# Row sums of the softmax in the third layer turned on TensorE, and evacuations given to ScalarE

## Chip, cores and metric

The kernel runs on one core of one Trainium2 chip. The metric is the device time of one execution in microseconds (us); before the change the median of three runs is 2798.11 us.

## What is computed

Four token mixers over one sequence of 1024 positions with 1024 features, all in float32: gated linear attention, dilated sliding-window attention, differential attention and multi-head latent attention, each followed by gating, an output projection and a residual with its norm. The third is the one that matters most here:

```python
def _diff_attention(h, positions, w_in, lam..., subln_g, w_out, lambda_init):
    q, k, v, z = split(h @ w_in)               # 8 heads, q and k of 2 x 64, v of 128
    q, k = _rope(q, positions), _rope(k, positions)
    ...
        sc = einsum('bqhcd,bkhcd->bhcqk', qb, k) * scale
        p = softmax(sc, axis=-1)
        p = p[:, :, 0] - lam * p[:, :, 1]
        o = einsum('bhqk,bkhd->bqhd', p, v)
    o = _rmsnorm(o, subln_g) * (1.0 - lambda_init)
    return (o * silu(z)) @ w_out
```

Layers three and four scale and shift their input by `silu(c) @ ada_w + ada_b` and multiply by a gate from the same product.

## The kernel before

Every matmul of float32 data is split into a high and a low part, and three products (high by high, low by high, high by low; L165 to L167) are added in PSUM. TensorE's order of work is written out by hand: the main loop of a layer issues its own matmuls and, by a credit in ns, gives time to a list of small units (`Fill`) that prepare what comes next: projections of the next head (`u_q`, `u_k`), gates (`u_gate`, L250), values (`u_v`) and the modulation (`u_ada`, L557: eight multiply-adds on VectorE, L575 and L577, over a 2 MB weight piece, then two matmuls against ones at L583). The other engines' order is set by the framework's scheduler from the data dependences and a simulated time. SyncE (SP in the profile) issues all transfers, in order.

A unit's result leaves PSUM by a copy: the gates' on ScalarE for the first half of the sequence and on VectorE for the second (L254), the second layer's values on VectorE and ScalarE in turn (L959), the third layer's likewise (L1285), the fourth layer's low-rank projections on VectorE (L1485). Before each of the layers two to four a stage (`pre`) runs such units with no attention beside them. Value weights come as `wvraw`, are cast on ScalarE (L204, `wvhi`) and their low part made on VectorE (`wvlo`, L150).

The third layer (`da`) walks 8 heads by 8 query tiles of 128 rows, 64 iterations `i`, and two more that finish. An iteration turns the probabilities of tile i-2 (`attend`, L1240: eight PE transposes of 128x128, copied to `PTh` on ScalarE and `PTl` on VectorE), finishes the softmax difference of tile i-1 (`combine`, L1440 to L1443: reciprocal, factor, P[0] + factor P[1]), computes the scores of tile i (L1420), their maxima on VectorE (L1424) and exponentials on ScalarE (L1426). On every odd iteration `pv` (L1358) multiplies a pair of tiles by the values, writes the unnormalised output to DRAM (`d_o`) and `norm` (L1377) writes a row of sums of squares (`d_ms`).

The outputs are not divided by the softmax sum: that goes into the RMS norm. For this the sum of the first softmax, `dsum` (128 rows on partitions, one column for each tile), is written to DRAM (`d_dn`), four columns at a time, and `factors` (L1245) loads sums of squares and softmax sums back as 128x4 pieces (`vr`), for all heads at once, and makes the factors on VectorE by an integer guess and four Newton steps (L1254 to L1265). It is called from `norm` at two places (head 6 last tile, head 7 second pair) and once in the boundary behind the layer. The write is

```python
nc.sync.dma_start(self.dnd[h][:, half(t // 4)].rearrange("o (f p) -> (o p) f", p=128), dsum[:, t - 3:t + 1])
```

in `combine`, that is, 512 elements of 4 bytes, each to an address of its own.

Of the kernel before, what the change touches and what calls it, by code (L numbers as in the profile page):

```python
# [8 lines left out]
F32 = mybir.dt.float32  # L9
# [128 lines left out]
class Kern:  # L138
# [111 lines left out]
    def u_gate(self, h, src, pool, halves=(0, 1), w=None):  # L250

        def evac(hf, s, ps):
            z = self.wp.tile([128, 512], F32, name="zt", bufs=2)
            (self.nc.vector.tensor_copy if hf else self.nc.scalar.copy)(z, ps)  # L254
            self.nc.sync.dma_start(self.zd[h][hf], z)
        return self.u_t(("g", h, halves[0]), (src, h), evac, halves=halves, w=w)
# [6 lines left out]
    def build(self):  # L263
        tc, nc, A = self.tc, self.nc, self.A
        with ExitStack() as ctx:
# [9 lines left out]
            self.ones = cp.tile([128, 128], F32, name="ones")  # L275
            self.ones_r = cp.tile([128, 128], F32R, name="ones_r")
            self.cv = cp.tile([128, 4], F32, name="cv")
# [6 lines left out]
            nc.vector.memset(self.ones_r.bitcast(F32), 1.0)  # L284
# [34 lines left out]
    def gla(self):  # L319
        tc, nc, A = self.tc, self.nc, self.A  # L320
        V, S, G, T = nc.vector, nc.scalar, nc.gpsimd, nc.tensor
        with ExitStack() as ctx:
# [22 lines left out]
            def u_g(h, halves=(0, 1)):  # L345
                return self.u_gate(h, "gla_wg", gp, halves)
# [334 lines left out]
    def boundary(self, name, wo, res, res_out, warm, ln=None, gate=None, mod=None, normed=False):  # L681
# [151 lines left out]
        for hf, off, n in parts:  # L833
            s = slice(hf * 512 + off, hf * 512 + off + n)
            for kt in range(2 if hf == 0 else 6 if final else 3, 8) if off == 0 else ():
                if normed and hf == 0 and kt == 7:
                    self.factors(bo, [(7, 1)])
# [90 lines left out]
    def swa(self, before):  # L928
# [6 lines left out]
        with ExitStack() as ctx:  # L935
# [13 lines left out]
            with tc.tile_pool(name="swv", bufs=1, reuse_waits="tile") as vp:  # L949
# [7 lines left out]
                def u_vs(g, sts):  # L957
                    def evac(st, ps):
                        (S.copy if st % 2 else V.tensor_copy)(Vt[g][:, st, :], ps)  # L959
# [225 lines left out]
            def after(h, g):  # L1185
# [13 lines left out]
                if g == 2:  # L1199
                    if h == 2:  # L1200
                        fill.add(u_kk(1, 0))
                    fill.add(self.u_gate(h, "swa_wg", ap, (0, 1) if h > 2 else (1,)))
# [42 lines left out]
    def factors(self, pool, hs):  # L1245

        nc, V = self.nc, self.nc.vector
# [6 lines left out]
        V.scalar_tensor_tensor(e, e, 128.0 * 1e-6, e, op0=OP.mult, op1=OP.mult)  # L1254
        V.tensor_tensor(t, t, e, op=OP.add)
        V.tensor_scalar(t, t, 1.0 / 128.0, None, op0=OP.mult)

        yi = y.bitcast(I32)
        V.tensor_scalar(yi, t.bitcast(I32), 1, None, op0=OP.logical_shift_right)
        V.tensor_scalar(yi, yi, -1.0, float(0x5f3759df), op0=OP.mult, op1=OP.add)  # L1260
        V.tensor_scalar(t, t, -0.5, None, op0=OP.mult)
        for _ in range(4):
            V.tensor_tensor(e, y, y, op=OP.mult)
            V.tensor_tensor(e, e, t, op=OP.mult)
            V.scalar_tensor_tensor(y, e, 1.5, y, op0=OP.add, op1=OP.mult)  # L1265
        for n, (g, hf) in enumerate(hs):
            nc.sync.dma_start(flat(self.rsd[g], hf), y[:, 4 * n:4 * n + 4])

    def da(self, before):
# [3 lines left out]
        with ExitStack() as ctx:  # L1273
            with tc.tile_pool(name="dav", bufs=1, reuse_waits="tile") as vp:
# [8 lines left out]
                def evac_v(pr, st, ps):  # L1283
                    t = vp.tile([128, 256], F32, name="vs", bufs=3)
                    (S.copy if st % 2 else V.tensor_copy)(t, ps)  # L1285
# [11 lines left out]
                with tc.tile_pool(name="ada1", bufs=1, side="right", reuse_waits="tile") as gp:  # L1297
                    ada = [self.u_ada(gp, *it) for it in ((1, 0), (1, 1), (1, 2), (1, 3), (0, 4), (0, 5))]
                    pre.add(u_vs(0, range(4, 8)), u_vs(1, range(4, 5)), ada[0], u_vs(1, range(5, 8)), ada[1], u_vs(2, range(0, 4)), ada[2], u_vs(2, range(4, 8)), ada[3], u_vs(3, range(0, 4)), ada[4], u_vs(3, range(4, 8)), ada[5])
# [50 lines left out]
            zs = [self.u_gate(h, "da_wz", dp, (hf,)) for hf, h in [(1, h) for h in range(3)] +  # L1350
# [7 lines left out]
            def pv(qb):  # L1358
                h, qb4 = divmod(qb, 4)
                s = slice(qb4 % 2 * 256, qb4 % 2 * 256 + 256)  # L1360
                o = self.mmp.tile([128, 256], F32, name="mm")
                vh, vl = VH[h]
                PTh, PTl = PT.pop(qb)
                for j in range(8):
# [6 lines left out]
                nc.sync.dma_start(self.od[h][qb4 // 2][:, s], y)  # L1371
                sq = dp.tile([128, 256], F32, name="sq")
# [3 lines left out]
            def norm(h, qb4, sq):  # L1376
# [5 lines left out]
                if (h, qb4) in FACT:  # L1382
                    self.factors(dp, FACT[h, qb4])

            FACT = {(6, 3): [(h, hf) for h in range(7) for hf in range(2)], (7, 1): [(7, 0)]}
            nrm, comb = None, []
            for i in range(64 + 2):
# [7 lines left out]
                if comb:  # L1395
                    comb.pop()()
                if i < 64:
# [37 lines left out]
                    if nrm and j % 2:  # L1435
                        norm(*nrm)
# [3 lines left out]
                    def combine(dn=dn, d0=d0, P=P, h=h, t=t, dsum=dsum):  # L1440
# [340 lines left out]
```

## Time and profile before

| | before |
|---|---|
| median of 3 runs | 2798.11 us (2795.3 to 2800.18) |
| the profiled execution: its time | 2794.63 us |
| its span in the profile | 2792.9 us |
| mean granted TensorE clock, as a share of the full one | 0.985 |
| busy: TensorE / VectorE / ScalarE / GpSimd | 95% / 68% / 48% / 11% |

The profile has a page for the whole span and views of any stretch: what ran when on an engine, how long it sat idle before and what released it, busy times and granted clock by window. An idle time in square brackets stands just ahead of the instruction that it ends before.

### The profile page before, as it was taken

How to read it: one execution, taken by the hardware profiler on the slowest of the kernel's cores; microseconds unless marked ns; L12 is line 12 of the kernel's file. 1: busy time of each engine (PE TensorE's matmuls, PEld its weight loads, DVE VectorE, ACT ScalarE, POOL GpSimd, SP SyncE). 2: the span in 40 equal slices, each digit the busy share in tenths (PEclk: the TensorE clock that was granted, in tenths of full speed). 3: DMA queues.
4: the chain of work that ended last, by engine and by line, in shares of the span. 5: the costliest groups of instructions: out<-in, count | busy, mean ns of one | idle time of the engine just before them, and what ended most of it. 6: DMA issues, size and time to landing. Idle time of an engine off the chain costs nothing.

```text
span 2792.9 us, 39308 instructions
## 1 busy us (share of the span) xinstructions
PE 2660.9 (95%) x14788; PEld 2234.5 (80%) x14788; DVE 1890.0 (68%) x3478; ACT 1349.2 (48%) x2492; POOL 314.6 (11%) x224
## 2 busy tenths in 40 slices
PE   8999999998999999988999999998799899999998
PEld 7889988887778878776897877786578688888878
DVE  7776547567666666667657788886576627777785
ACT  5444345426344434347515766765445415554563
POOL 0000000000000000000015656664000000000000
PEclk9999999999999999999999999999799999999999
DMA  5310155654111111154642432342275220100143
GB/s 206 107 43 32 49 180 182 210 176 144 50 42 50 46 47 53 50 185 145 228 165 74 63 67 61 66 55 62 90 266 170 68 70 23 33 27 29 39 172 110
DMA packets 163926, 274.70 MB, mean 98 GB/s; under 512 B 32948, under 2 KB 82388, under 8 KB 162072
## 3 DMA queue, kind: packets, MB, share of 16 engines
q1 hardware_dynamic: 163736, 272.19, 31.7%
q8 instruction: 116, 1.90, 0.3%
q14 instruction: 74, 0.61, 0.1%
HBM read 195.48 MB, written 66.17 MB: 94 GB/s over the span
## 4 chain that ended last, share of the span: by engine, by line
PE 67%; DVE 14%; DMA 7%; ACT 7%; issue 3%; SPq 1%; POOL 1%; ACTq 0%; DVEq 0%; POOLq 0%
PE mm L165 14%; PE mm L166 14%; PE mm L167 14%; PE pt L1240 3%; PE sc L1420 3%; PE sc L1657 2%; PE sc L1049 2%; PE lv L489 1%; PE pt L1153 1%; PE sc L166 1%; PE sc L165 1%; PE sc L167 1%; DVE den L1424 1%; PE mm L1623 1%; DVE wlo L150 1%
## 5 line engine op out<-in xcount | busy, mean ns | idle before, releaser
L165 PE MATMUL mm<-xh,whi 128*128 128x512 f32 x1456 | 613.3, 421 | 18.0 <-DVE t L911 6.0
L167 PE MATMUL mm<-xh,wlo 128*128 128x512 f32 x1456 | 574.0, 394 | 2.5 <-POOL wlo L150 1.6
L166 PE MATMUL mm<-xl,whi 128*128 128x512 f32 x1456 | 574.0, 394 | 1.7 <-DVE xl L150 1.7
L165 PEld LDWEIGHTS mm<-xh,whi 128*128 128x128 f32 x1456 | 277.6, 191 | 75.5 <-DVE t L911 7.3
L167 PEld LDWEIGHTS mm<-xh,wlo 128*128 128x128 f32 x1456 | 275.8, 189 | 64.4 <-POOL wlo L150 2.5
L166 PEld LDWEIGHTS mm<-xl,whi 128*128 128x128 f32 x1456 | 277.6, 191 | 52.9 <-DVE xl L150 4.0
L150 POOL TENSOR_TENSOR wlo<-wraw,whi 128x1024 fp32r<-128x1024 f32 x29 | 70.6, 2435 | 1334.9 <-ACT whi L192 1332.9
L165 PE MATMUL mm<-wvhi,xh 128*128 128x256 f32 x704 | 204.6, 291 | 4.8 <-DVE V L959 3.0
L192 ACT CAST whi<-wraw 128x1024 fp32r<-128x1024 f32 (+2 forms) x141 | 135.9, 964 | 138.3 <-PE mm L166 128.9
L167 PE MATMUL mm<-wvhi,xl 128*128 128x256 f32 x704 | 199.2, 283 | 0.1
L166 PE MATMUL mm<-wvlo,xh 128*128 128x256 f32 x704 | 198.6, 282 | 0.0
L1426 ACT ACTIVATE P<-sc,den 128x1024 f32<-128x1024 f32 x128 | 142.9, 1117 | 113.4 <-DVE den L1424 112.8
L1424 DVE TENSOR_REDUCE den<-sc 128x1 f32<-128x1024 f32 x128 | 153.5, 1212 | 3.5 <-PE sc L1420 3.5
L150 DVE TENSOR_TENSOR wlo<-wraw,whi 128x1024 fp32r<-128x1024 f32 (+2 forms) x113 | 123.5, 1093 | 43.8 <-ACT whi L192 40.7
L1043 ACT ACTIVATE P<-P,nm 128x128 f32<-128x128 f32 (+1 forms) x192 | 84.9, 443 | 124.5 <-DVE nm L1041 124.2
L165 PEld LDWEIGHTS mm<-wvhi,xh 128*128 128x128 f32 x704 | 134.0, 190 | 9.9 <-DVE V L959 3.2
L166 PEld LDWEIGHTS mm<-wvlo,xh 128*128 128x128 f32 x704 | 134.5, 191 | 1.3 <-issue 1.0
L167 PEld LDWEIGHTS mm<-wvhi,xl 128*128 128x128 f32 x704 | 133.9, 190 | 0.4 <-DVE xl L150 0.4
L165 PE MATMUL mm<-oh,xh 128*128 128x512 f32 (+1 forms) x336 | 126.1, 375 | 0.3 <-ACT oh L796 0.3
L166 PE MATMUL mm<-ol,xh 128*128 128x512 f32 (+1 forms) x336 | 124.2, 370 | 2.0 <-DVE ol L150 2.0
L167 PE MATMUL mm<-oh,xl 128*128 128x512 f32 (+1 forms) x336 | 123.7, 368 | 0.0
L1053 DVE CUSTOM_DVE_ANT_0 P<-sc,band 128x128 f32<-128x128 f32 (+1 forms) x192 | 59.6, 348 | 71.5 <-PE sc L1049 71.1
(355 smaller groups left out, 6124.5 us busy)
## 6 DMA issues: line engine op xcount, KB each, us to landing
xa<-in_ada_w SPq DMA_DIRECT2D x12, 2048.0 KB
d_z<-zt SPq DMA_DIRECT2D x64, 256.0 KB
oh<-d_z SPq DMA_DIRECT2D x64, 256.0 KB
ol<-d_o SPq DMA_DIRECT2D x64, 256.0 KB
d_r<-X SPq DMA_DIRECT2D x48, 256.0 KB
wraw<-in_swa_wq SPq DMA_DIRECT2D x24, 512.0 KB
res<-d_r SPq DMA_DIRECT2D x40, 256.0 KB
zt<-zt SPq DMA_DIRECT2D x160, 64.0 KB
```

What stands on the lines that cost most here:

```text
L150: eng.tensor_tensor(out, src, hi.bitcast(F32), op=OP.subtract)
L165: mm(ps, l[0], r[0], start=first, stop=False)
L166: mm(ps, l[0], r[1], start=False, stop=False)
L167: mm(ps, l[1], r[0], start=False, stop=last)
L192: nc.scalar.copy(hi, raw)
L1043: S.activation(p[:, off:off + w_], p[:, off:off + w_], AF.Exp, bias=nm[:, g, b:b + 1], scale=scale, accum_out=stat(h, g, 1, b))
L1049: T.matmul(sc[:, b % 2, :w_], q[:, b * 128:b * 128 + 128], k[:, k0:k0 + w_], start=True, stop=True)
L1053: V.tensor_tensor_reduce(p[:, off:off + w_], sc[:, b % 2, :w_], mk, 1.0, NEG, op0=OP.add, op1=OP.max, accum_out=stat(h, g, 0, b))
L1240: nc.tensor.transpose(pt[:, i, :], P[:, (4 * j + i) * 128:(4 * j + i) * 128 + 128], self.ident)
L1420: T.matmul(sc[c][:, s], QS[h][c][r, q0:q0 + 128], (KL[h] if k else KH[h][c])[r, s], start=first, stop=not first)
L1424: V.tensor_reduce(dn[:, 2 + c:3 + c], sc[c], AX, OP.max, negate=True)
L1426: S.activation(p, sc[c], AF.Exp, bias=dn[:, 2 + c:3 + c], accum_out=dn[:, 1:2] if c else d0)
```

## The change

Seven edits:

1. `dsum` is no longer written as it stands. `combine` puts it on a list `due`; at the head of the next `pv` TensorE transposes the four columns into four rows (a tile of their own in the PSUM bank that `pv` uses), ScalarE copies them to `dr`, and a transfer of four rows of 512 bytes goes out behind that of `d_o`. This happens 16 times.
2. `factors` issues its loads at once and returns the arithmetic as a function; the loop calls that two iterations later (in the boundary at once).
3. The gates' copies are ScalarE's for both halves in the preparation of the fourth layer (eight more copies); elsewhere `act=False` keeps the turn.
4. All value copies of the second layer (12 of 24 move) and of the third (16 of 32) are ScalarE's.
5. So are the 10 copies of the fourth layer's low-rank projections.
6. The six modulation units before the third layer stand after 8, 11, 14, 17, 20 and 24 row tiles of the values instead of 5, 8, 12, 16, 20 and 24; the last one before the fourth stands behind two more gates.
7. One tile of ones serves as float32 and as its split form.

```diff
-    def u_gate(self, h, src, pool, halves=(0, 1), w=None):
+    def u_gate(self, h, src, pool, halves=(0, 1), w=None, act=True):
...
-            (self.nc.vector.tensor_copy if hf else self.nc.scalar.copy)(z, ps)
+            (self.nc.scalar.copy if act or not hf else self.nc.vector.tensor_copy)(z, ps)
...
-                        (S.copy if st % 2 else V.tensor_copy)(Vt[g][:, st, :], ps)
+                        S.copy(Vt[g][:, st, :], ps)
...
         for n, (g, hf) in enumerate(hs):
             nc.sync.dma_start(t[:, 4 * n:4 * n + 4], flat(self.msd[g], hf))
             nc.sync.dma_start(e[:, 4 * n:4 * n + 4], flat(self.dnd[g], hf))
-        V.scalar_tensor_tensor(e, e, 128.0 * 1e-6, e, op0=OP.mult, op1=OP.mult)
-        V.tensor_tensor(t, t, e, op=OP.add)
...
+        def rest():
+            V.scalar_tensor_tensor(e, e, 128.0 * 1e-6, e, op0=OP.mult, op1=OP.mult)
+            V.tensor_tensor(t, t, e, op=OP.add)
...
+        return rest
...
-                    (S.copy if st % 2 else V.tensor_copy)(t, ps)
+                    S.copy(t, ps)
...
-                    pre.add(u_vs(0, range(4, 8)), u_vs(1, range(4, 5)), ada[0], u_vs(1, range(5, 8)), ada[1], u_vs(2, range(0, 4)), ada[2], u_vs(2, range(4, 8)), ada[3], u_vs(3, range(0, 4)), ada[4], u_vs(3, range(4, 8)), ada[5])
+                    pre.add(u_vs(0, range(4, 8)), u_vs(1, range(4, 8)), ada[0], u_vs(2, range(0, 3)), ada[1], u_vs(2, range(3, 6)), ada[2], u_vs(2, range(6, 8)), u_vs(3, range(0, 1)), ada[3], u_vs(3, range(1, 4)), ada[4], u_vs(3, range(4, 8)), ada[5])
...
-                o = self.mmp.tile([128, 256], F32, name="mm")
+                bank = self.mmp.tile([128, 512], F32, name="mm")
+                o, d = bank[:, :256], bank[0:4, 256:384]
...
+                if due:
+                    T.transpose(d, due[0][2], self.ident)
...
+                if due:
+                    g, hf, _ = due.pop()
+                    r = dp.tile([128, 128], F32, name="dr")
+                    S.copy(r[0:4], d)
+                    nc.sync.dma_start(self.dnd[g][:, half(hf)].rearrange("o (f p) -> (o f) p", p=128), r[0:4])
...
+                if facts and facts[0][0] <= i:
+                    facts.pop()[1]()
...
-                        norm(*nrm)
+                        if f := norm(*nrm):
+                            facts.append((i + 2, f))
...
-                            nc.sync.dma_start(self.dnd[h][:, half(t // 4)].rearrange("o (f p) -> (o p) f", p=128),
-                                              dsum[:, t - 3:t + 1])
+                            due.append((h, t // 4, dsum[:, t - 3:t + 1]))
...
-                        V.tensor_copy(raw[key, hf][:, c, :], ps)
+                        S.copy(raw[key, hf][:, c, :], ps)
...
-                pre.add(self.u_ada(p0, 1, 5, 1), *[self.u_gate(h, "mla_wz", p0) for h in range(3, 8)])
+                late = [self.u_gate(h, "mla_wz", p0) for h in range(3, 8)]
+                pre.add(*late[:2], self.u_ada(p0, 1, 5, 1), *late[2:])
```

The scheduler makes of it the following on three queues (the line numbers are each kernel's own). SyncE near the end of the third layer, before (`wraw` are weights, `d_z` gates, `d_o` outputs):

```order
L1251 DMA vr<-d_ms 128x4
L1445 DMA d_dn<-dsum 128x4x1
L255 DMA d_z<-zt 128x512
L1252 DMA vr<-d_dn 128x4
...
L1381 DMA d_ms<-sq 1x256
L179 DMA wraw<-in_w_out 128x1024
L1251 DMA vr<-d_ms 128x4
L1445 DMA d_dn<-dsum 128x4x1
L1371 DMA d_o<-y 128x256
```

and now:

```order
L1378 DMA d_o<-y 128x256
L1383 DMA d_dn<-dr 4x128
L1252 DMA vr<-d_dn 128x4
L255 DMA d_z<-zt 128x512
L1393 DMA d_ms<-sq 1x256
L179 DMA wraw<-in_w_out 128x1024
L1251 DMA vr<-d_ms 128x4
L1378 DMA d_o<-y 128x256
```

The writes of `d_dn` moved from right behind a load of `vr` from `d_ms` to a place behind `d_o`, one load of `vr` from `d_dn` follows each at once, and nothing of `d_dn` stands beside the load from `d_ms` now.

VectorE in the iterations at the end of head 6 and the start of head 7, where the first call of `factors` lies, before (56 columns are 14 pieces of four):

```order
L1441 RECIPROCAL den<-den 128x1
L1442 SCALAR_TENSOR_TENSOR den<-den,nlam,dsum 128x1
L1443 SCALAR_TENSOR_TENSOR P<-P,den 128x1024
L1254 SCALAR_TENSOR_TENSOR vr<-vr 128x56
L150 TENSOR_TENSOR PTl<-pt,PTh 128x4x128
...
L150 TENSOR_TENSOR PTl<-pt,PTh 128x4x128
L1424 TENSOR_REDUCE den<-sc 128x1
L1255 TENSOR_TENSOR vr<-vr 128x56
L1441 RECIPROCAL den<-den 128x1
L1256 TENSOR_SCALAR vr<-vr 128x56
L1442 SCALAR_TENSOR_TENSOR den<-den,nlam,dsum 128x1
```

and now:

```order
L1438 TENSOR_REDUCE den<-sc 128x1
L1256 SCALAR_TENSOR_TENSOR vr<-vr 128x56
L1456 RECIPROCAL den<-den 128x1
L1457 SCALAR_TENSOR_TENSOR den<-den,nlam,dsum 128x1
...
L150 TENSOR_TENSOR PTl<-pt,PTh 128x4x128
L1438 TENSOR_REDUCE den<-sc 128x1
L1257 TENSOR_TENSOR vr<-vr 128x56
L1456 RECIPROCAL den<-den 128x1
L1258 TENSOR_SCALAR vr<-vr 128x56
L1457 SCALAR_TENSOR_TENSOR den<-den,nlam,dsum 128x1
```

The first step (L1254, now L1256) moved two reciprocals, that is two iterations, later, and stands behind the maxima; the second (L1255, now L1257) has the place that it had, right ahead of the next reciprocal.

ScalarE in the preparation of the second layer, where the first values of it are copied, before:

```order
L254 COPY zt<-mm 128x512
L741 CAST xh_70<-X 128x512 x2
L204 CAST wvhi<-wvraw 128x512
L959 COPY V_4095<-mm 128x256
L204 CAST wvhi<-wvraw 128x512
L959 COPY V_4095<-mm 128x256
L755 ACTIVATE rs<-stat 1x512
L959 COPY V_4096<-mm 128x256 x2
```

and now:

```order
L254 COPY zt<-mm 128x512
L740 CAST xh_70<-X 128x512 x2
L958 COPY V_4093<-mm 128x256
L204 CAST wvhi<-wvraw 128x512 x2
L958 COPY V_4093<-mm 128x256 x3
L958 COPY V_4094<-mm 128x256
L754 ACTIVATE rs<-stat 1x512
L958 COPY V_4094<-mm 128x256 x3
```

The copies that VectorE made are in ScalarE's queue, and the second value copy is now behind two casts of value weights instead of behind one.

## Rows read from the trace of the kernel before

**Rows 1.** The page: busy time, share of the span and instructions of each engine.

```profile
PE 2660.9 (95%) x14788; PEld 2234.5 (80%) x14788; DVE 1890.0 (68%) x3478; ACT 1349.2 (48%) x2492; POOL 314.6 (11%) x224
```

**Rows 2.** Windows: stretch, its length, busy time (instructions) by engine, PEclk, DMA share, GB/s.

```profile
1360.00:1400.00 40.00, 36.34 (x287) 34.62 (x286) 28.47 (x47) 9.20 (x19) 0.00 (x0) 1.00 0.77 278
1500.00:1890.00 390.00, 388.91 (x2193) 311.35 (x2191) 320.00 (x379) 269.10 (x503) 254.03 (x180) 1.00 0.36 62
1890.00:2020.00 130.00, 101.31 (x505) 78.42 (x504) 78.19 (x131) 63.51 (x119) 27.39 (x19) 0.85 0.23 67
```

**Rows 3.** Timeline of VectorE, end of the third layer: start, length, instruction [idle before, releaser].

```profile
1928.10 0.22 DVE L1254 SCALAR_TENSOR_TENSOR vr<-vr 128x56 f32<-128x56 f32 x1 [7.03 <-DMA vr<-d_dn]
...
1962.55 0.22 DVE L1255 TENSOR_TENSOR vr<-vr 128x56 f32<-128x56 f32 x1 [9.08 <-DMA vr<-d_ms]
...
1998.66 0.16 DVE L1255 TENSOR_TENSOR vr<-vr 128x4 f32<-128x4 f32 x1 [6.66 <-DMA vr<-d_ms]
```

**Rows 4.** Timeline of TensorE, same stretch: the instructions behind its longest idle times.

```profile
1903.42 0.50 PE L165 MATMUL mm<-xh,whi 128*128 128x512 f32 x1 [2.51 <-ACT y L1370]
...
1928.97 1.11 PE L1240 MATMUL pt<-ident,P 128*128 128x128 f32 x4 [5.44 <-DVE PTl L150]
...
1965.95 0.66 PE L1240 MATMUL pt<-ident,P 128*128 128x128 f32 x4 [3.91 <-DVE PTl L150]
...
1967.89 1.08 PE L1240 MATMUL pt<-ident,P 128*128 128x128 f32 x4 [1.29 <-DVE vr L1264]
...
1999.47 1.97 PE L1240 MATMUL pt<-ident,P 128*128 128x128 f32 x8 [6.11 <-DVE PTl L150]
```

**Rows 5.** Windows cut to stretches in which TensorE's granted clock was 0.50.

```profile
1926.00:1936.20 10.20, 6.53 (x20) 4.56 (x21) 6.76 (x11) 3.68 (x7) 0.00 (x0) 0.50 0.23 65
1967.00:1977.20 10.20, 9.31 (x32) 7.12 (x33) 9.99 (x22) 7.47 (x13) 0.00 (x0) 0.50 0.27 79
1994.30:2004.50 10.20, 5.03 (x23) 4.81 (x24) 4.85 (x21) 1.17 (x2) 0.00 (x0) 0.50 0.01 2
2229.80:2236.60 6.80, 5.93 (x12) 4.03 (x13) 3.01 (x6) 0.62 (x1) 0.00 (x0) 0.50 0.37 119
```

**Rows 6.** Timeline of SyncE, end of the third layer: issues of transfers.

```profile
1911.60 0.24 SPq L1381 DMA_DIRECT2D d_ms<-sq  x1
...
1914.35 0.32 SPq L1251 DMA_DIRECT2D vr<-d_ms  x1
...
1915.26 0.37 SPq L1445 DMA_DIRECT2D d_dn<-dsum  x1
...
1925.52 0.32 SPq L1252 DMA_DIRECT2D vr<-d_dn  x1
...
1952.72 0.37 SPq L1251 DMA_DIRECT2D vr<-d_ms  x1
...
1953.15 0.43 SPq L1445 DMA_DIRECT2D d_dn<-dsum  x1
```

**Rows 7.** Timeline of TensorE, preparation of the fourth layer: behind idle times.

```profile
2219.53 0.47 PE L165 MATMUL mm<-xh,whi 128*128 128x512 f32 x1 [1.70 <-DVE zt L254]
...
2221.17 0.50 PE L167 MATMUL mm<-xh,wlo 128*128 128x512 f32 x1 [0.94 <-DVE wlo L150]
...
2230.67 2.08 PE L583 MATMUL mm<-xb,ones 128*128 128x512 f32 x2 [4.22 <-DVE xb L577]
```

**Rows 8.** Timeline of TensorE, preparation of the third layer: behind its longest idle time.

```profile
1381.44 1.10 PE L583 MATMUL mm<-xb,ones 128*128 128x512 f32 x2 [2.94 <-DVE xb L577]
```

**Rows 9.** Timeline of ScalarE (ACT) and TensorE, preparation of the second layer.

```profile
525.69 1.14 ACT L741 CAST xh<-X 128x512 fp32r<-128x512 f32 x2
...
532.75 0.62 ACT L204 CAST wvhi<-wvraw 128x512 fp32r<-128x512 f32 x1 [1.70 <-DMA wvraw<-in_swa_wv]
...
531.10 0.39 PE L165 MATMUL mm<-wvhi,xh 128*128 128x256 f32 x1 [0.52 <-ACT V L959]
```

**Rows 10.** Timeline of TensorE: eight transposes together at the full clock.

```profile
1990.32 1.04 PE L1240 MATMUL pt<-ident,P 128*128 128x128 f32 x8
```

More of the change, by code (lines that the diff above doesn't have):

```diff
@@ L274, in build @@
             self.ident = cp.tile([128, 128], F32, name="ident")
-            self.ones = cp.tile([128, 128], F32, name="ones")
             self.ones_r = cp.tile([128, 128], F32R, name="ones_r")
+            self.ones = self.ones_r.bitcast(F32)
             self.cv = cp.tile([128, 4], F32, name="cv")
@@ L283, in build @@
             nc.vector.memset(self.ones, 1.0)
-            nc.vector.memset(self.ones_r.bitcast(F32), 1.0)
             for i, v in enumerate((1.0, 1e-5, 1e-6, 0.0)):
@@ L345, in u_g @@
             def u_g(h, halves=(0, 1)):
-                return self.u_gate(h, "gla_wg", gp, halves)
+                return self.u_gate(h, "gla_wg", gp, halves, act=False)
             nc.sync.dma_start(self.vecs, A["vecs"])
@@ L836, in boundary @@
                 if normed and hf == 0 and kt == 7:
-                    self.factors(bo, [(7, 1)])
+                    self.factors(bo, [(7, 1)])()
                 gated(hf, kt)
@@ L1201, in after @@
                         fill.add(u_kk(1, 0))
-                    fill.add(self.u_gate(h, "swa_wg", ap, (0, 1) if h > 2 else (1,)))
+                    fill.add(self.u_gate(h, "swa_wg", ap, (0, 1) if h > 2 else (1,), act=False))
             for g in range(3):
@@ L1252, in factors @@
             nc.sync.dma_start(e[:, 4 * n:4 * n + 4], flat(self.dnd[g], hf))
-        V.scalar_tensor_tensor(e, e, 128.0 * 1e-6, e, op0=OP.mult, op1=OP.mult)
-        V.tensor_tensor(t, t, e, op=OP.add)
[L1256 to L1267, printed above, removed]
+        def rest():
+            V.scalar_tensor_tensor(e, e, 128.0 * 1e-6, e, op0=OP.mult, op1=OP.mult)
+            V.tensor_tensor(t, t, e, op=OP.add)
+            V.tensor_scalar(t, t, 1.0 / 128.0, None, op0=OP.mult)
+            yi = y.bitcast(I32)
+            V.tensor_scalar(yi, t.bitcast(I32), 1, None, op0=OP.logical_shift_right)
+            V.tensor_scalar(yi, yi, -1.0, float(0x5f3759df), op0=OP.mult, op1=OP.add)
+            V.tensor_scalar(t, t, -0.5, None, op0=OP.mult)
+            for _ in range(4):
+                V.tensor_tensor(e, y, y, op=OP.mult)
+                V.tensor_tensor(e, e, t, op=OP.mult)
+                V.scalar_tensor_tensor(y, e, 1.5, y, op0=OP.add, op1=OP.mult)
+            for n, (g, hf) in enumerate(hs):
+                nc.sync.dma_start(flat(self.rsd[g], hf), y[:, 4 * n:4 * n + 4])
+        return rest
     def da(self, before):
@@ L1349, in da @@
             fill = Fill()
-            zs = [self.u_gate(h, "da_wz", dp, (hf,)) for hf, h in [(1, h) for h in range(3)] +
+            zs = [self.u_gate(h, "da_wz", dp, (hf,), act=False) for hf, h in [(1, h) for h in range(3)] +
                   [(hf, h) for h in range(3, 8) for hf in range(2)]]
@@ L1382, in norm @@
                 if (h, qb4) in FACT:
-                    self.factors(dp, FACT[h, qb4])
+                    return self.factors(dp, FACT[h, qb4])
             FACT = {(6, 3): [(h, hf) for h in range(7) for hf in range(2)], (7, 1): [(7, 0)]}
-            nrm, comb = None, []
+            nrm, comb, due, facts = None, [], [], []
             for i in range(64 + 2):
```

## Prediction

> **What bounds the kernel.** I read the page first: TensorE is busy for 95% of the span [rows 1], so what can be won is its idle time and the time that it spends at a lower clock. The windows say where: in the body of the third layer TensorE is busy for 388.91 of 390 us at full clock, in the layer's end for only 101.31 of 130, at 0.85 of the clock [rows 2]. The timelines of TensorE and VectorE of that end come next. TensorE waits five times, for 2.51, 5.44, 3.91, 1.29 and 6.11 us, mostly for `PTl`, which VectorE makes [rows 4]; VectorE at those times stands in front of the arithmetic of `factors` for 7.03, 9.08 and 6.66 us, for a load of `vr` [rows 3]. SyncE's timeline shows why these loads are late: beside each is a write of `d_dn` in 4-byte elements. Issued at 1915.26, it lets the load that reads it go only at 1925.52, 10.3 us later; a row of `d_ms` (1 KB) issued at 1911.60 does so by 1914.35, in 2.75 us [rows 6]. The load of 1925.52 itself is in by 1928.10 [rows 3], in 2.6 us, whereas the one of 1952.72, with a write of `d_dn` 0.43 us behind it [rows 6], ends VectorE's wait at 1962.55 [rows 3], after 9.8. After the long waits the clock sits at 1.2 GHz for 10.2 us each [rows 5].
>
> **Term by term**, against the profiled execution's 2794.63 us.
>
> *End of the third layer.* The write becomes four rows of 512 bytes. No row shows one; the nearest is the `d_ms` row, so I take 2.75 us for it, with 10.3 (no gain) as the other end. The first step now stands two iterations behind its old place and its load is issued an iteration ahead of it: the 7.03 go, and TensorE's 5.44 with them. The second step keeps its place, so its wait stays in kind: the load from `d_ms` goes out at 1952.7, where VectorE arrived about a microsecond later (9.08 before 1962.55 is 1953.47). With 2.6 us for the load and up to 2 for the weights ahead of it VectorE waits 2 to 4 us instead of 9.08. TensorE had lost 3.91 + 1.29 = 5.2 of these 9.08, so it can bear 3.9; I leave 1.0 and count 4.2. At the third place it bore almost nothing (6.11 of 6.66): with a wait of 1.7 left, 4.4 go. The 2.51 of 1903 are not a wait for `vr`; VectorE and ScalarE were late there behind loads that SyncE held back while it waited for an earlier write. Bounds 0 and 2.51, half: 1.25. Sum of idle time 5.44 + 4.2 + 4.4 + 1.25 = 15.3.
>
> The clock: work at half of it takes twice its time, so a low stretch costs half its busy time: 6.53/2 = 3.3, 9.31/2 = 4.7 and 5.03/2 = 2.5 [rows 5]. The first two follow the first two stalls and go; the last lies where the queue of other work runs out, so I count half of it, 1.2. Sum 9.2. Together **-24.5**; bounds -8.7 (first stall and its clock only) and -31 (nothing left).
>
> *Transposes.* Sixteen are added on TensorE, in the stretch where it never idles, so all of their time counts. Eight of full size take 1.04 us together [rows 10], 0.13 each; four at half clock 1.11 [rows 4], 0.28 each. 16 times these: 2.1 and 4.5; **+3.0**, between, since each stands alone between other work. Their input was made over an iteration before; no wait. The 16 copies to `dr` lie on ScalarE, busy for 269 of 390 us there [rows 2], and nothing on TensorE reads them: nothing, as long as that third of its time is free. If each delayed an exponential by its own length of some 0.4 us, that would be 6.
>
> *Preparation of the fourth layer.* The moved modulation unit finds its sum made: 4.22 go [rows 7], and half of the 5.93 at low clock, 3.0 [rows 5]. With the gate copies on ScalarE, VectorE isn't late for the 1.70 and the 0.94 [rows 7]. **-9.8**, bounds -5 and -10. The low-rank copies go from an engine that was late to one that waits for it: 0.
>
> *Preparation of the third layer.* Two row tiles more lie ahead of the second unit: the 2.94 [rows 8] can go, but the units then follow each other every three tiles, and the one behind may be late. Bounds 0 and -2.94; **-2.0**.
>
> *Preparation of the second layer.* A loss. The first copy of values now waits for the casts that end at 526.83; the second stands behind two casts of weights, of which the last ends at 532.75 + 0.62 = 533.37, since it waits for a load. TensorE, which resumed at 531.10 behind that copy, can do so at about 533.7 [rows 9]: **+2.6**; the lower bound is 0, if it is made up where later loads are late anyway.
>
> Edit 7 is one memset less at the start, under the first loads: 0.
>
> Sum -24.5 + 3.0 - 9.8 - 2.0 + 2.6 = -30.7. The profiled execution is 3.5 us under the median 2798.11; against the median this is **2767 us**.
>
> **Rivals.** *A: the loads stay late.* The second step has its old place, and the load has a weight load right ahead of it on SyncE. If that is what holds it, not the 4-byte write, only the first stall (5.44 + 3.3) and the 1.25 go: -10.0 + 3.0 - 9.8 - 2.0 + 2.6 = -16.2, **2782 us**. For it: the loads still come in 16-byte pieces. Against it: the load of 1925.52, of the same pieces, took 2.6 us. The Trainium skill, page "DMA: Bandwidth & Descriptors", section Specifications, gives 512 B as the least transfer at full rate, below which the engine reads, modifies and writes. By that rule, if it holds for loads, the loads would stay slow and this rival's sum stand; the 2.6 us disagree, and no run here shows it yet. Chance 0.17.
>
> *B: ScalarE becomes the late engine; slower.* 28 value copies move behind casts that wait for loads, in stages where transfers take 0.77 of the DMA time [rows 2]. The first two cost 2.6, so 1.3 each. If the other 26 paid this too, 33.8 come on top: +3.1, **2801 us**; it turns slower from about 1.2 each. For it: casts and copies share one queue in order. Against it: in that stage ScalarE is busy for 9.20 of 40 us [rows 2], and only a copy right behind a waiting cast pays. Chance 0.07.
>
> *C: the whole end heals.* Without the writes the third place has no wait, the 1.0, 1.7, 1.2 and 1.3 that I left go too, and the small waits of the last iterations shrink: some 8 us more, **2759 us**. Chance 0.16.
>
> *D: the gains cancel* (the transposes' 4.5, copies in the way of the exponentials, 6, and A): within a few us of 2795. Chance 0.06.
>
> **The numbers.** The forecast has 0.54 for 2762 to 2776. The range reaches from 2753, below C, to 2788, above A. About 0.2%, 5.6 us, is what a measurement can tell from no change: faster takes the forecast, A and C, 0.87; the same, D, 0.06; slower, B, 0.07.
>
> **What would show it.** VectorE's wait at L1256 gone and at L1257 2 to 4 us and under 2 (rows of `vr`); a load behind `d_dn` issued within 3 us of the write; full clock from 1890 to 1980; no wait of TensorE for `xb` before the fourth layer; one of about 3 us in the second's preparation. Waits of over 6 us at L1257 would mean A, and waits of TensorE for `vs` or `V` in many tiles B; then the forecast is wrong.

## The result, and the profile after

| | before | changed |
|---|---|---|
| median | 2799.14 us (4 runs, 2795.3 to 2800.56) | 2771.18 us (4 runs, 2769.0 to 2773.91) |
| the profiled execution | 2794.63 us | 2769.0 us |
| its span | 2792.9 us | 2767.2 us |

The ratio is 0.9903, with a 95% interval of 0.9886 to 0.992: 28 us faster, where 31 were forecast, and 2771 lies inside the range. Of the runs in the experiments one execution, of the fourth layer's preparation alone, took 4323.15 us at a granted clock of 0.557 and is left out of its median.

Where it went is read by following the same instruction through both traces:

| what starts | before, us | changed, us | difference | gained or lost since |
|---|---|---|---|---|
| first value matmul before the second layer | 518.47 | 518.90 | +0.4 | |
| first matmuls after that preparation | 616.23 | 618.77 | +2.5 | +2.1 |
| sixth matmul of the second layer's output projection | 1219.37 | 1219.61 | +0.2 | -2.3 |
| first reciprocal of the third layer | 1485.96 | 1489.63 | +3.7 | +3.5 |
| its 53rd | 1889.70 | 1896.14 | +6.4 | +2.7 |
| output projection of the third layer | 2018.19 | 1998.06 | -20.1 | -26.5 |
| first transposes of the fourth layer | 2317.9 | 2292.5 | -25.4 | -5.3 |
| end of the span | 2792.9 | 2767.2 | -25.7 | -0.3 |

So the end of the third layer gave about all of the gain, and the three preparations together, where most of the edits lie, next to nothing. A stage of a few us is known only roughly from one pair of traces. By the first matmul of the second layer's output projection (1211.82 and 1213.28) the entries -2.3 and +3.5 read -1.1 and +2.2; and a second trace of the changed kernel, from the experiments, has +1.3 and +0.9 for the preparations of the second and third layer, -28.1 for the end and -6.8 for the preparation of the fourth.

The page's line of busy times, which answers to [rows 1], and the windows, which answer to [rows 2], with one of a stretch at half clock (granted clock 0.50) in the second layer's preparation:

```profile
PE 2651.0 (96%) x14804; PEld 2228.6 (81%) x14804; DVE 1871.8 (68%) x3431; ACT 1368.2 (49%) x2554; POOL 313.5 (11%) x224
```

```profile
1500.00:1890.00 390.00, 387.34 (x2200) 310.07 (x2199) 319.61 (x376) 268.72 (x514) 249.19 (x176) 1.00 0.22 61
1890.00:2000.00 110.00, 98.36 (x539) 78.42 (x538) 82.81 (x137) 68.03 (x130) 33.48 (x25) 0.95 0.27 78
524.80:531.60 6.80, 5.33 (x25) 5.33 (x26) 5.61 (x9) 3.35 (x7) 0.00 (x0) 0.50 0.96 298
```

TensorE is busy for 10 us less in all, because less of its work is done at half clock: in stretches at 0.50 it is busy for 42.6 us, against 60.9, and half of the difference is 9.2. In the body of the third layer the transfers take 0.22 of the DMA engines' time where they took 0.36, for 61 GB/s against 62. The pieces of 4 bytes are not themselves that difference: by the trace's records of single packets those of 4 bytes took 0.012 of the engines' time before, while a packet of 4096 bytes took 0.578 us on average and takes 0.229 now. So other transfers' packets took longer beside the pieces. In the layer's end TensorE is busy for 98.36 of 110 us, against 101.31 of 130.

VectorE's timeline there, which answers to [rows 3], and SyncE's, which answers to [rows 6]:

```profile
1940.02 0.22 DVE L1256 SCALAR_TENSOR_TENSOR vr<-vr 128x56 f32<-128x56 f32 x1
...
1949.81 0.22 DVE L1257 TENSOR_TENSOR vr<-vr 128x56 f32<-128x56 f32 x1 [2.60 <-DMA vr<-d_ms]
...
1976.84 0.16 DVE L1256 SCALAR_TENSOR_TENSOR vr<-vr 128x4 f32<-128x4 f32 x1 [2.23 <-DMA vr<-d_dn]
...
1978.17 0.16 DVE L1257 TENSOR_TENSOR vr<-vr 128x4 f32<-128x4 f32 x1 [0.84 <-DMA vr<-d_ms]
```

```profile
1906.05 0.29 SPq L1383 DMA_DIRECT2D d_dn<-dr  x1
...
1907.44 0.32 SPq L1252 DMA_DIRECT2D vr<-d_dn  x1
...
1935.90 0.29 SPq L1383 DMA_DIRECT2D d_dn<-dr  x1
...
1938.20 0.32 SPq L1252 DMA_DIRECT2D vr<-d_dn  x1
```

The first step waits for nothing; the second for 2.60 us instead of 9.08; at the third place, where VectorE waited 6.66 us, it waits 2.23 and 0.84. A load behind a write of `d_dn` goes out 1.4 and 2.3 us after it, where it took 10.3. Of TensorE's waits [rows 4] two are left that stand before transposes:

```profile
1963.93 1.06 PE L1239 MATMUL pt<-ident,P 128*128 128x128 f32 x8 [1.02 <-DVE den L1456]
...
1980.26 1.97 PE L1239 MATMUL pt<-ident,P 128*128 128x128 f32 x8 [1.68 <-DVE PTl L150]
```

The preparations are another matter. TensorE in that of the fourth layer, which answers to [rows 7], first its wait for a low-rank copy before, then two of the changed kernel:

```profile
2176.28 0.50 PE L165 MATMUL mm<-xh,whi 128*128 128x512 f32 x1 [2.43 <-DVE lraw L1485]
```

```profile
2156.63 0.80 PE L165 MATMUL mm<-xh,whi 128*128 128x512 f32 x1 [3.09 <-ACT lraw L1499]
...
2202.32 0.50 PE L167 MATMUL mm<-xh,wlo 128*128 128x512 f32 x1 [2.31 <-DVE wlo L150]
```

The 4.22 us for the modulation unit are gone, as forecast, but a low-rank copy is late by 3.09 and `wlo` by 2.31. And in those of the third and the second layer, which answer to [rows 8, 9], TensorE, VectorE and ScalarE by turns; the last fence has TensorE's wait of the kernel before in the second layer's:

```profile
1379.42 0.74 ACT L1288 COPY vs<-mm 128x256 f32<-128x256 f32 x2 [2.95 <-DMA d_v<-vs]
...
1379.84 0.39 PE L165 MATMUL mm<-wvhi,xh 128*128 128x256 f32 x1 [1.68 <-ACT vs L1288]
...
1395.36 1.25 ACT L204 CAST wvhi<-wvraw 128x512 fp32r<-128x512 f32 x2 [2.44 <-DMA wvraw<-in_da_wv]
...
1396.01 0.69 DVE L150 TENSOR_TENSOR wvlo<-wvraw,wvhi 128x512 fp32r<-128x512 f32 x1 [1.70 <-ACT wvhi L204]
...
1401.92 1.91 PE L582 MATMUL mm<-xb,ones_r 128*128 128x512 f32 x2 [3.70 <-DVE xb L576]
...
526.27 0.58 PE L165 MATMUL mm<-wvhi,xh 128*128 128x256 f32 x1 [4.23 <-ACT zt L254]
```

```profile
524.57 0.38 PE L165 MATMUL mm<-wvhi,xh 128*128 128x256 f32 x1 [2.96 <-DVE V L959]
```

A copy of values on ScalarE waits 2.95 us for the store that frees its buffer, and TensorE 1.68 for the copy; the second modulation unit is late by 3.70, since on VectorE its sum stands behind a low part that waits for its cast, which waits for its load. In the second layer's preparation TensorE's longest wait was 2.96 us before, for VectorE's copy of values; it is 4.23 now, for a copy on ScalarE, and the clock stays at half for 6.8 us behind it.

### The profile page after: what moved, and what is told of

The parts are those of the page before. It is cut to its first block, busy times and chain, and to the rows that moved or that the text cites. A ratio compares the mean times of both kernels' runs of the same rounds, so it can differ in the third digit from the quotient of the medians.

```text
span 2767.2 us, 39358 instructions
## 1 busy us (share of the span) xinstructions
PE 2651.0 (96%) x14804; PEld 2228.6 (81%) x14804; DVE 1871.8 (68%) x3431; ACT 1368.2 (49%) x2554; POOL 313.5 (11%) x224
## 4 chain that ended last, share of the span: by engine, by line
PE 70%; DVE 14%; ACT 6%; DMA 6%; issue 3%; SPq 1%; POOL 0%; DVEq 0%; ACTq 0%; POOLq 0%
PE mm L165 15%; PE mm L166 15%; PE mm L167 14%; PE pt L1239 3%; PE sc L1434 3%; PE sc L1672 2%; PE sc L1048 2%; PE lv L488 1%; PE pt L1152 1%; PE sc L166 1%; PE mm L1638 1%; PE sc L165 1%; PE mm L1636 1%; PE mm L1635 1%; PE sc L167 1%
```

## Experiments

The main theory was that the 4-byte writes hold the loads, and that this is the whole gain; the rivals that the loads were late for the weights ahead of them, that the end of the layer also needed VectorE relieved, and that small pieces of any kind are as slow. All runs have the kernel before beside them on the same chip.

The arithmetic's call two iterations later (edit 2) has no run of its own: the kernel with the turned write has the same instructions in the same order on all five engines with that edit and without it, and so has the one with the 4-byte write. The scheduler orders VectorE by its simulated time, not by where the call stands. In the traces the first step stands behind the 58th reciprocal in the changed kernel and with the turned write alone, which lacks edit 2, and behind the 56th before: the later write moved it. Edit 7 frees 512 bytes per partition, which `dr` takes: the layer's pool had no room for it otherwise.

**The turned write alone** (edits 1 and 7):

```diff
+                if due:
+                    T.transpose(d, due[0][2], self.ident)
...
+                    S.copy(r[0:4], d)
+                    nc.sync.dma_start(self.dnd[g][:, half(hf)].rearrange("o (f p) -> (o f) p", p=128), r[0:4])
```

> The kernel before with the turned write alone (edits 1 and 7; the arithmetic of factors is called at once as before). Theory: the 4-byte writes held the loads, so this part alone brings nearly all of the end of the third layer: about -25 us there, +2.5 us for 16 transposes, -22 us in all, ratio 0.992; the waits at the first two steps of factors fall from 7.0, 9.1 and 6.7 us to 3 us and less. Rival: the end also needed the copies taken from VectorE or the deferred call; then -10 us or less, ratio 0.996 or above, and a wait of over 5 us is left.

Measured: 0.9916 (0.9902 to 0.9929), 2772.08 against 2795.13 us, 23 us faster. The theory holds. VectorE at the two places of the second step:

```profile
1947.55 0.22 DVE L1254 TENSOR_TENSOR vr<-vr 128x56 f32<-128x56 f32 x1 [2.60 <-DMA vr<-d_ms]
...
1973.29 0.16 DVE L1254 TENSOR_TENSOR vr<-vr 128x4 f32<-128x4 f32 x1 [0.23 <-DMA vr<-d_ms]
```


**The second layer's value copies alone.**

```diff
-                        (S.copy if st % 2 else V.tensor_copy)(Vt[g][:, st, :], ps)
+                        S.copy(Vt[g][:, st, :], ps)
```

> The kernel before with the second layer's value copies on ScalarE alone (a part of edit 4). Theory: 2.5 to 3 us are lost in that layer's preparation, with half clock behind a TensorE wait of 4.2 us at 526, and given back by the next boundary, so 0 to +1 us, ratio 1.000. Rival: the loss stays, +2.6 us, ratio 1.001, and the next boundary starts later by that much.

Measured: 1.002 (1.0008 to 1.0032), 4 us slower by the medians: neither, and more than was expected of the stage. The trace has the wait of 4.24 us in the preparation, as expected, and something that the profile of the kernel before does not have: a fourth long wait near the end of the third layer, ahead of the three known ones. SyncE, VectorE and TensorE there:

```profile
1879.20 2.42 SPq L919 DMA_DIRECT2D zt<-zt  x4
...
1882.20 0.38 SPq L1445 DMA_DIRECT2D d_dn<-dsum  x1
```

```profile
1891.40 0.69 DVE L922 TENSOR_TENSOR zt<-zt,C 128x512 f32<-128x512 f32 x1 [9.11 <-DMA vr<-d_dn]
...
1896.29 1.11 PE L1240 MATMUL pt<-ident,P 128*128 128x128 f32 x4 [4.31 <-DVE PTl L150]
```

VectorE's instruction multiplies the tile whose four loads went out just ahead of the write of `d_dn`, and waits 9.11 us. So a 4-byte write can hold VectorE at this place too; the next two runs show the same, ending at 1887.37 and 1886.68, and the changed kernel, which has no 4-byte write, waits at most 0.40 us here in two traces. The kernel before has its write as close behind these loads and waits 1.08 us; what decides between the two isn't shown. Nor is the fourth wait what makes this kernel slower in all: from the 50th reciprocal to the output projection it takes 152.65 us, the kernel before 152.40, since the later waits are shorter. Of the 3.0 us that this trace is longer, 1.9 lie ahead of the stage (its first value matmul starts at 520.37) and 2.6 in it, and 1.5 are given back behind it; so what the copies cost beyond these 2.6 stays open.

**The third layer's preparation alone** (copies on ScalarE, units moved).

```diff
-                    (S.copy if st % 2 else V.tensor_copy)(t, ps)
+                    S.copy(t, ps)
...
-                    pre.add(u_vs(0, range(4, 8)), u_vs(1, range(4, 5)), ada[0], u_vs(1, range(5, 8)), ada[1], ...
+                    pre.add(u_vs(0, range(4, 8)), u_vs(1, range(4, 8)), ada[0], u_vs(2, range(0, 3)), ada[1], ...
```

> The kernel before with the third layer's value copies on ScalarE and its modulation units moved, alone (parts of edits 4 and 6). Theory, from the changed kernel's trace: slower by 3 to 4 us (ratio 1.0012), with TensorE waits of 1.7 us for a copy on ScalarE that waits for a store and of 3.7 us for the second unit, and a stretch of half clock. Rival, as predicted: faster by 2 us (ratio 0.9993), the changed kernel's loss having come from the other edits.

Measured: 1.0026 (1.0016 to 1.0036), 5 us slower by the medians. TensorE in that stage:

```profile
1376.15 0.39 PE L165 MATMUL mm<-wvhi,xh 128*128 128x256 f32 x1 [2.54 <-ACT vs L1285]
...
1398.04 1.52 PE L583 MATMUL mm<-xb,ones 128*128 128x512 f32 x2 [3.52 <-DVE xb L577]
```

The two waits of the changed kernel are here without its other edits, 6.06 us in place of 2.94 and 0.66 before: the loss is this part's own. The end of the layer, with the fourth wait in it, adds to it: 154.25 us from the 50th reciprocal to the output projection, against 152.40.

**The fourth layer's preparation alone** (edits 3 and 5, the later unit).

```diff
-                        V.tensor_copy(raw[key, hf][:, c, :], ps)
+                        S.copy(raw[key, hf][:, c, :], ps)
...
+                pre.add(*late[:2], self.u_ada(p0, 1, 5, 1), *late[2:])
```

> The kernel before with the fourth layer's preparation alone changed (edits 3 and 5 and the other part of 6). Theory, from the changed kernel's trace: -6 us (ratio 0.998): the wait of 4.2 us for the modulation unit and its half clock go, waits of 3.1 us for a low-rank copy (with 3.4 us of half clock) and 2.3 us for wlo come. Rival, as predicted: -9.8 us (ratio 0.9965), if the changed kernel lost the rest elsewhere.

Measured: 0.9977 (0.9967 to 0.9987), 2790.44 against 2795.13 us. The theory's size, and in the trace the stage itself, from the third layer's output projection to the fourth's first transposes, takes 294.57 us instead of 299.71; the rival's 0.9965 lies just outside the interval. The low-rank copy's wait, and the fourth wait again, on VectorE:

```profile
1886.68 0.69 DVE L922 TENSOR_TENSOR zt<-zt,C 128x512 f32<-128x512 f32 x1 [9.86 <-DMA vr<-d_ms]
...
2174.67 0.80 PE L165 MATMUL mm<-xh,whi 128*128 128x512 f32 x1 [3.11 <-ACT lraw L1485]
```


**The changed kernel beside three cut versions.** The first is the changed kernel once more.

> The changed kernel itself again, beside the next three on one chip: 0.990 of the kernel before, about 2769 us.

Measured: 0.99 (0.9885 to 0.9915), 2767.61 us (2766.49 to 2768.76). The two waits of the third layer's preparation in this second trace:

```profile
1381.62 0.39 PE L165 MATMUL mm<-wvhi,xh 128*128 128x256 f32 x1 [2.22 <-ACT vs L1288]
...
1403.94 1.10 PE L582 MATMUL mm<-xb,ones_r 128*128 128x512 f32 x2 [2.45 <-DVE xb L576]
```

The second leaves the preparations of the second and third layer (copies and places of the units), and the call of `factors`, as they were; of its edit, the copies:

```diff
-                        S.copy(Vt[g][:, st, :], ps)
+                        (S.copy if st % 2 else V.tensor_copy)(Vt[g][:, st, :], ps)
...
-                    S.copy(t, ps)
+                    (S.copy if st % 2 else V.tensor_copy)(t, ps)
```

> The kernel before with the turned write, the one tile of ones and the fourth layer's preparation (edits 1, 3, 5, 7 and half of 6); the copies and units of the second and third layers' preparation and the call of factors as before. Theory: those parts cost 2 to 6 us in the changed kernel, so this is faster than it by that: 0.9895 to 0.988, about 2764 us. Rival: they cost nothing once the 4-byte writes are gone (their cost alone came with an extra stall at such a write); then the same as the changed kernel.

Measured: 0.9884 (0.987 to 0.9899), 2763.33 us (2761.37 to 2764.84). No run of the one reaches into those of the other: those parts cost 4.3 us by the medians, as the theory has it, and the changed kernel is better without them.

The third gives the low-rank copies back to VectorE:

```diff
-                        S.copy(raw[key, hf][:, c, :], ps)
+                        V.tensor_copy(raw[key, hf][:, c, :], ps)
```

> The previous one with the fourth layer's low-rank copies on VectorE as before (edit 5 undone). Theory: the wait of 3.1 us for such a copy goes back to 2.4, and the half clock behind it goes: 1 to 2.5 us faster than the previous one. Rival: VectorE is late again for other work of that stage, same or slower by up to 2 us.

Measured: 0.9888 (0.9874 to 0.9903), 2764.74 us: the same. TensorE's wait is shorter again, 2.40 us instead of the 3.12 of the second version, but here 3.4 us of half clock begin at it, as in the first trace of the changed kernel, and its first matmul takes 0.80 us instead of 0.50. Behind the longer wait of the second version the clock stays full. The second version, then this one:

```profile
2151.93 0.50 PE L165 MATMUL mm<-xh,whi 128*128 128x512 f32 x1 [3.12 <-ACT lraw L1492]
```

```profile
2151.60 0.80 PE L165 MATMUL mm<-xh,whi 128*128 128x512 f32 x1 [2.40 <-DVE lraw L1492]
```

Edit 5 is worth nothing that these runs can tell.

The fourth puts the third layer's units where the change has them, on top of the third:

```diff
-                    pre.add(u_vs(0, range(4, 8)), u_vs(1, range(4, 5)), ada[0], u_vs(1, range(5, 8)), ada[1], ...
+                    pre.add(u_vs(0, range(4, 8)), u_vs(1, range(4, 8)), ada[0], u_vs(2, range(0, 3)), ada[1], ...
```

> The previous one with the third layer's modulation units where the change puts them (edit 6 whole), its copies on both engines as before. Theory: the 2.9 and 0.7 us waits for the first two units go and one of 3 to 4 us for the second comes, since its sum stands on VectorE behind a low part that waits for a load of weights: 0 to +1 us against the previous one. Rival, as predicted: 2 us faster, the copies on ScalarE alone having done the harm.

Measured: 0.9895 (0.9878 to 0.9911), 2766.49 us (2765.21 to 2770.58), 1.8 above the third version: not clearly slower, and not the 2 us faster that the rival has. TensorE:

```profile
1391.99 0.38 PE L165 MATMUL mm<-wvhi,xh 128*128 128x256 f32 x1 [1.82 <-ACT vs L1284]
...
1404.42 1.10 PE L582 MATMUL mm<-xb,ones_r 128*128 128x512 f32 x2 [2.05 <-DVE xb L576]
```

The second unit is late by 2.05 us with the copies on both engines, where the third version has 3.70 before the first unit and 0.66 before the second, so the order alone makes that wait; there are waits for `vs` beside it, of 1.82 here and 1.58 at 1380. Moving the units traded two waits for three.

**Each 4-byte write made twice.** The second goes to DRAM that is not read.

```diff
+                            nc.sync.dma_start(self.spare[h][:, half(t // 4)].rearrange("o (f p) -> (o p) f", p=128),
+                                              dsum[:, t - 3:t + 1])
```

> The kernel before with each 4-byte write of the softmax sums made twice, the second time to DRAM that nobody reads. Theory (the 4-byte elements are slow to be done with, and loads around them count as done only after them): the waits of VectorE at the first two steps of factors grow from 7.0, 9.1 and 6.7 us to 14 us or more each, and the time by 15 to 35 us. Rival (the loads are late for the weights ahead of them on SyncE): waits and time as before, within 3 us.

Measured: 2903.12 us beside 2797.55 (one run each), 105.6 us slower, three times the theory's upper end and no part of the rival. SyncE at the first step, and VectorE at all three places:

```profile
2015.93 0.37 SPq L1446 DMA_DIRECT2D d_dn<-dsum  x1
...
2016.35 0.50 SPq L1448 DMA_DIRECT2D d_sp<-dsum  x1
...
2025.14 0.33 SPq L1253 DMA_DIRECT2D vr<-d_dn  x1
```

```profile
2037.13 0.22 DVE L1255 SCALAR_TENSOR_TENSOR vr<-vr 128x56 f32<-128x56 f32 x1 [15.37 <-DMA vr<-d_dn]
...
2068.16 0.65 DVE L1256 TENSOR_TENSOR vr<-vr 128x56 f32<-128x56 f32 x1 [5.51 <-issue]
...
2103.90 0.16 DVE L1256 TENSOR_TENSOR vr<-vr 128x4 f32<-128x4 f32 x1 [5.59 <-DMA vr<-d_ms]
```

The load still goes out 9.2 us after the first write, but it counts as in only 12 us later, and VectorE waits 15.37 us instead of 7.03. The other two waits, which the theory has growing as well, fell, from 9.08 and 6.66 to 5.51 and 5.59. So the theory holds in the whole time and at the first step, and does not say how late each single load is. Most of the 105 us is in the body: from the 10th reciprocal to the 50th it takes 1948.94 - 1558.39 = 390.6 us, the kernel before 1865.79 - 1551.22 = 314.6. One write at a time is hidden there, two in a row are not.

**Pieces of 16 bytes.** The sums are written as they lie, four to a partition; the third layer's factors then use sums of other rows.

```diff
-                            nc.sync.dma_start(self.dnd[h][:, half(t // 4)].rearrange("o (f p) -> (o p) f", p=128),
+                            nc.sync.dma_start(self.dnd[h][:, half(t // 4)].rearrange("o (p f) -> (o p) f", f=4),
```

> The kernel before with the softmax sums written as 128 pieces of 16 bytes instead of 512 of 4 (at other addresses, so that the factors of the third layer use the sums of other rows). Theory: the cost goes with the number of pieces, so the write is done in a quarter of the time, 2.5 us more than a row, and waits fall to 2 to 4 us; the time like that of the turned write, -15 to -22 us. Rival: any write of pieces far under 512 bytes is as slow as one of 4: waits of 6 us and more, time as before.

Measured: 2773.7 us beside 2797.55 (one run each), 24 us faster. SyncE at the write ahead of the first step, and VectorE's waits for `vr` (us in total, times, longest):

```profile
1912.46 0.32 SPq L1445 DMA_DIRECT2D d_dn<-dsum  x1
...
1913.97 0.39 SPq L1252 DMA_DIRECT2D vr<-d_dn  x1
```

```profile
DVE vr L1255 <- DMA vr<-d_ms: 3.4, 2, 2.8
...
DVE vr L1254 <- DMA vr<-d_dn: 0.5, 1, 0.5
```

1.5 us from the write to the load behind it, and no wait over 2.8. The write stands where it stood, so neither its later place nor the transposes are needed. The rival is out: pieces of 16 bytes, 128 of them, do as well as four of 512. The gain needs no turning. In the body the transfers' share is 0.23, as with the turned write (0.22).

**Each transpose four times** on top of the turned write.

```diff
-                    T.transpose(d, due[0][2], self.ident)
+                    for _ in range(4):
+                        T.transpose(d, due[0][2], self.ident)
```

> The turned write alone, with each of its transposes made four times over into the same place (48 more on TensorE). Theory: one costs the 0.04 to 0.1 us by which the body of the third layer grew, +2 to +5 us against the turned write alone, all of it between the 10th and the 60th tile. Rival, as predicted: 0.13 to 0.28 each, +6 to +13 us.

Measured: 2773.27 us (one run), the turned write alone 2772.08. The 10th and the 50th reciprocal, first of the turned write alone and then of this kernel:

```profile
1555.63 0.17 DVE L1449 RECIPROCAL den<-den 128x1 f32<-128x1 f32 x1 [1.27 <-ACT P L1434]
...
1869.62 0.16 DVE L1449 RECIPROCAL den<-den 128x1 f32<-128x1 f32 x1 [1.27 <-ACT P L1434]
```

```profile
1549.77 0.17 DVE L1450 RECIPROCAL den<-den 128x1 f32<-128x1 f32 x1 [1.50 <-ACT P L1435]
...
1864.99 0.16 DVE L1450 RECIPROCAL den<-den 128x1 f32<-128x1 f32 x1 [1.27 <-ACT P L1435]
```

313.99 and 315.22 us for forty iterations, in which ten writes, so thirty transposes more: 1.23/30 = 0.04 us each. Four kernels without transposes, the one before among them, differ by 1.1 us over the same iterations (313.44 to 314.57), so 0.08 is possible and the rival's 0.13 is out. In the whole time, 1.2 us above the turned write alone, the run lies below the theory's +2 as well, though single executions of that kernel differ by 4.9.

**No transposes, and a right result:** 16-byte writes, and loads that gather in pieces of 4 bytes, with the fourth layer's preparation as changed.

```diff
+            for f in range(4):
+                nc.sync.dma_start(e[32 * f:32 * f + 32, 4 * n:4 * n + 4],
+                                  self.dnd[g][:, half(hf)].rearrange("o (q c f) -> (o f) q c", q=32, f=4)[f])
```

> No transposes: the softmax sums are written as 128 pieces of 16 bytes, and the loads of the factors gather them in pieces of 4 bytes (each load is four of 128 pieces), with the fourth layer's preparation as changed and the rest as before. Theory: only the writing of 4-byte pieces is slow, reading them is not; then as fast as the turned write with that preparation, 0.9884, about 2763 us, with waits for vr under 4 us. Rival: pieces of 4 bytes are slow in both directions, or the 48 issues more on SyncE hold up other loads: waits for vr of 5 us and more and 5 to 25 us slower than that.

Measured: 0.9879 (0.9859 to 0.99), 2761.38 us (2756.48 to 2763.91). VectorE at the second step:

```profile
1941.75 0.22 DVE L1257 TENSOR_TENSOR vr<-vr 128x56 f32<-128x56 f32 x1 [2.75 <-DMA vr<-d_ms]
```

Reading pieces of 4 bytes costs nothing that shows; writing them does. With the second cut version (0.9884), from which it differs by the way of the sums and edit 7, this is the best of all kernels here, and some 7 us below the changed one by the ratios (0.9879 and 0.9903), though the intervals overlap; the changed one has the second and third layer's copies besides.

## Why the prediction was right

**The end of the third layer** was forecast at -24.5 and gave -26.5. The mechanism is shown from both sides: the turned write alone brings 23 us of the 28, writing the same sums in 16-byte pieces from the old place brings 24, and doubling the 4-byte write more than doubles the wait at the first step. The step "VectorE waits 2 to 4 us instead of 9.08" was met with 2.60, and the 1.0 us that it left to TensorE with 1.02; "a wait of 1.7 left" with 2.23 and 0.84 one behind the other on VectorE, and 1.68 on TensorE. The 2.51, of which half was counted, went whole. Half clock fell from 10.2 us behind each long wait to stretches of 3.4 and 6.8 us in the last iterations, which were counted as staying in part; from 1890 to 1978.92 the clock is full. The lower bound, -31, doesn't come out of the terms: with nothing left of the waits and the half clock they give -29.7.

**Rival A** fell: the load has the weights ahead of it as before, in 16-byte pieces as before, and is in time. The 512 bytes of the Trainium skill ("DMA: Bandwidth & Descriptors", Specifications) are no line between slow and fast here: written pieces of 16 bytes (2773.7 us) did as well as rows of 512 (2772.08), and the measurement decides. The same page ("Queues, rings and completion order") says that a transfer's semaphore lands only after every earlier write of that DMA engine. The 15.37 us for a load issued behind two such writes agree with it.

The trace's records of packets and of semaphores show where the time lies. Each of these transfers raises its semaphore 16 times, and what waits for it goes on after the last. Of the write issued at 1953.15 before, the 512 pieces had gone out by 1955.73, but its semaphore was raised between 1959.21 and 1963.45. Of the load issued 0.43 us ahead of that write eight counts were in by 1955.82; the other eight came between 1957.49 and 1962.43, and VectorE's 9.08 us ended at 1962.55. In the second run the last load of the tile had 15 counts by 1883.07 and the last one at 1891.18, among those of the write (1888.45 to 1892.12), which ended VectorE's 9.11 us; before, that load had all 16 by 1880.16. So the pieces are not slow to be sent but slow to be counted as done, and a load beside them, issued ahead of them too, is late by the counts that come in with theirs.

**The transposes** were the term of +3.0, sized at 0.13 to 0.28 each from neighbours; they measured 0.04, at most 0.08, so 1.3 at most for sixteen. The body still grew by 2.7 us in the changed kernel, of which 2.6 lie between the 8th and 10th reciprocal; the kernel with four times the transposes does not have that step there, so they are not its cause. Every kernel with one transpose for each write has it, and those with 16-byte writes do not. What its cause is stays open; the trace shows VectorE's two instructions behind the 8th reciprocal longer than usual (2.01 and 2.40 us instead of 0.22 and 1.28), beside GpSimd's. That the sum's +3.0 was met is luck.

**The fourth layer's preparation**, -9.8 forecast, gave -5.3. The steps that failed are "the low-rank copies go from an engine that was late to one that waits for it: 0", and that VectorE "isn't late" for `wlo`: the first wait went from 2.43 to 3.09, and in place of the 1.70 and 0.94 came 2.31, since `wlo` stands behind the same products for `qa` as the copy did. Of the 3.0 for half clock some 1.4 came back, since 3.4 us of it stand behind the low-rank copy now, in this trace; in the second one they don't, and the stage gave -6.8. The direction was right, and the unit's 4.22 went.

**The third layer's preparation**, -2.0 forecast, gave +3.5 in this trace and +0.9 in the second: wrong in sign, and outside its bounds of 0 and -2.94. The 2.94 stood before the first unit, not the second, with three more row tiles ahead of it now, not two, and it did go. "The one behind may be late" was written and then bounded at no loss. It was late by 3.70 (2.45 in the second trace), with half clock behind it, and a copy that waits for a store came on top, which is rival B in one place.

**The second layer's preparation**, +2.6 forecast, lost 2.1 in the stage (1.3 in the second trace). The step was another than the one named: TensorE does not wait for the second copy of values, at 533.7, but for a copy on ScalarE at 526.27, 4.23 us instead of 2.96, with half clock behind it. Whether the loss stays is not settled: in this trace about even is reached at the next projection, but the part alone was 4 us slower.

In sum, by the first pair of traces: end 2 us better, transposes and body as summed though not for the reason given, the three preparations -2.0 (-5.3 + 3.5 + 2.1 - 2.3 given back) instead of -9.2. The one large term carried the forecast; the small ones, each right in where to look, were wrong in what would be late next.

Rival B, slower in all, was far off, but its mechanism shows in the runs of single parts: the second and third layer's copies (the latter with the moved units) cost 4 and 5 us with the 4-byte writes in place, and 4.3 together without them. Rival D's terms, added up, come to 2789 us and not to about 2795.

## What to carry to other kernels

A write of single elements to DRAM was paid for by others here: look at what is loaded around it, and at the time from the write to the first load behind it. Before moving data through another engine to make such pieces larger, try to write them as they lie and to gather on the reading side; here 16 bytes were enough. And a wait that an edit removes is worth what the next one behind it leaves: for preparation stages with several engines in turn, that next one has to be named and sized, or the term be set near zero.

## What was not expected of the hardware

Writes in 4-byte pieces and reads in 4-byte pieces are not alike: 512 pieces written held a load behind them for some 10 us, while 128 at a time read, 64 times over, left the time at 2761.38 us. The written pieces had gone out within some 3 us of their issue; it was their semaphore that took the rest. And a second such write behind each of the sixteen cost 105.6 us more, where the sixteen alone cost about 23: the body of the third layer, which hid one at a time, could not hide two.
